# RWKV's bonus product is written into the quarter's own output columns, and the wait for the gate of the second quarter back is dropped

## The chip, the core and the metric

The kernel runs on one core of a Trainium2 chip. A core has five engines that each work through a queue of their own in order: TensorE (PE, matrix products and transposes), VectorE (DVE), ScalarE (ACT), GpSimd (POOL) and SyncE (SP, which here only starts transfers). They wait for one another through semaphores. The metric is device time in microseconds (us) of one execution; lower is better. Several executions are timed and their median is compared. One more execution is recorded by the profiler, and durations and waits are read from that one.

## The reference

One layer of a hybrid recurrent trunk is applied to a prompt of 1024 tokens and, with states that are handed in, to 8 sample sequences of one token each. An input projection feeds three groups of heads: RWKV-7 (6 heads of 64), HGRN2 (6 heads of 64) and RG-LRU (256 channels). Their outputs go side by side through an output projection, a residual sum and an MLP of width 4096. The change touches the last lines of RWKV-7:

```
def step(S, inp):
    rt, wt, kt, vt, kkt, at = inp
    sa = jnp.einsum('bhvk,bhk->bhv', S, -kkt)
    S = S * wt[:, :, None, :] + sa[..., None] * (kkt * at)[:, :, None, :] + vt[..., None] * kt[:, :, None, :]
    return S, jnp.einsum('bhvk,bhk->bhv', S, rt)
...
gn = ((out - mean) * lax.rsqrt(var + GN_EPS)).reshape(B, T, c) * ln_w + ln_b
bonus = (jnp.sum(r_h * k_h * r_k, -1, keepdims=True) * v_h).reshape(B, T, c)
return (gn + bonus) * g, S_T
```

So the output of a token is the normalised scan output plus the bonus (a scalar per head times v), all times the gate g. The bonus needs r, k and v only, and neither the scan nor the gate.

## The kernel before, in words

Channels lie on the 128 partitions, tokens along the free axis. A dense product is made of three float32r products (high by high, high by low, low by high), named `in`, `out`, `up` and `dn` after the projection. The tile `mix[k]` (128 channels, all tokens) holds the layer's input first; once a half of the tokens is normalised and split into high and low parts, the same columns take the output of the head groups (RWKV has `mix[0]` to `mix[2]`), and later the residual stream.

The tokens of the prompt are taken in two halves of 512. RWKV cuts these once more: a *quarter* is 256 tokens of one pair of heads, in four *chunks* of 64. There are 12 quarters, numbered q = 0 to 11 in the order half, pair, quarter of the half (`PARTS`). A quarter named `1_0` on PE rows is half 1, first quarter. Four generators work on it:

- `rw_operands(q)` (line 515 on) makes the operands: decay, normalised keys, transposed keys and values (`vT`, `bt`, `kt`), and last, behind `yield D8`, the bonus: a product of PE (`bonus`), then a multiplication by v on DVE into the tile `bo`. It then releases the quarter's inputs and signals `A2`.
- `rw_inverse(q)` waits for `A2` and builds the inverse of a triangular matrix for each chunk (`sc`, `W`, `Y`), then signals `B`. Two streams share the quarters, even and odd.
- `rw_chain(q)` waits for `B` and carries the state through the four chunks: three dependent products a chunk (`ch` from `st,az`, from `rh,yz`, from `mv,bt`), each followed by a small DVE operation (lines 714, 718, 727). Then come 48 small products for the quarter's output, and it signals `C`.
- `rw_finish(q)` waits for `C`, normalises, transposes (`oT`), adds the bonus (line 772, which reads `bo` and writes `mix`), multiplies by the gate (`gate` on PE, line 779 on DVE) and signals `P`.

Beside these run HGRN2 (`hgrn`, which also does the sample part), RG-LRU (`lru`), and as the *filler* the dense products of the input projections and of the output projection (`projections`, `out_proj`). Near its end the filler waits for the last streams: the columns of `mix[2]` and `mix[5]` are split last (`KS`), and the key `("end",)` stands in front of them.

PE's order is written out by `weave`: it keeps a clock of its own, with a cost for each product and a delay (`D1`, `D2` and so on) after each step of a stream, takes whichever stream is due, and lets the filler have the rest. The order of the other engines is set by a scheduler of the tile framework, which looks at priorities (`PRI`).

The buffer `bo` has two copies. The line `if q >= 2: yield ("P", q - 2)` keeps `rw_operands` from asking for a third before the second quarter back has used its own and has gone through its gate. Until then this stream does nothing else, so the operands of the next quarter wait as well.

Of the kernel before, what the change touches and what calls it, by code (L numbers as in the profile page):

```python
# [17 lines left out]
P = 128  # L18
# [7 lines left out]
HT = 512  # L26
HW = HT + NB
QT = 256
# [24 lines left out]
def kernel(ctx: ExitStack, tc: tile.TileContext, i, o):  # L53
# [18 lines left out]
    def mm(out, lhsT, rhs, start=True, stop=True):  # L72
        n, m = rhs.free_size(), lhsT.free_size()
        now[0] += n / 2400 if rhs.dtype == F32R else 0.19 if n < 16 else max(n, m) / (600 if m > 64 else 800)
        PE.matmul(out, lhsT, rhs, start=start, stop=stop)  # L75

    def tr(out, in_, idn):
        now[0] += 0.11
        PE.transpose(out, in_, idn)
# [3 lines left out]
    def bank_o(name):  # L83

        while now[0] < o_busy[0]:
            yield o_busy[0] - now[0]
        return ps("o", name)

    def used_o(delay=L_O):
        o_busy[0] = now[0] + delay  # L90

    def ev(key, delay=1.5):
        done[key] = now[0] + delay
# [51 lines left out]
    mix = [mixp.tile([P, TP], F32, name=f"mix{k}") for k in range(KT)]  # L145
# [39 lines left out]
    def vec(name, k, n=1):  # L185
        return vt[:, at[name] + k:at[name] + k + n]
# [66 lines left out]
    def head_inv_root(sq, n, name, floor, tmp):  # L253

        pc = yield from bank_o(f"pc_{name}")
        nt = n // P
        for t in range(nt):
            mm(pc[:, 2 * t:2 * t + 2], sq[:, t * P:(t + 1) * P], bones2)
        used_o()
        a = small.tile([P, 2 * nt], F32, tag="ir_kk", name=f"ir_{name}", bufs=1)  # L260
        V.tensor_scalar(a, pc[:, :2 * nt], floor, None, op0=ALU.max)
        rpow(a)

        V.tensor_copy(tmp.rearrange("p (x c) -> p x c", c=64), bc(a[:, :, None], [P, 2 * nt, 64]))
        yield D1
        pb = yield from bank_o(f"pb_{name}")
        for t in range(nt):
            tr(pb[:, t * P:(t + 1) * P], tmp[:, t * P:(t + 1) * P], ident)
        used_o()
        return pb[:, 0:n]  # L270
# [231 lines left out]
    def w2(tag, n, bufs=2, name=None):  # L502
        return rwp.tile([P, QT], F32, tag=tag, name=f"{name or tag}_{n}", bufs=bufs)
# [7 lines left out]
    def twice(ap):  # L511

        return bc(ap.rearrange("p (c t) -> p c t", t=C)[:, :, None, :], [P, ap.shape[1] // C, 2, C])

    def rw_operands(q):

        j, hf, qt = PARTS[q]
        n = f"{j}_{hf}_{qt}"
        q0 = qt * QT
        qs = slice(q0, q0 + QT)  # L520
        jc = slice(j * P, (j + 1) * P)
        yield ("lora", hf)
        yield ("rkv", j, hf)
        xwa, _ = lora[hf]
        r, k, v = rkv[j, hf]

        def ck(ap):
            return ap.rearrange("p (c t) -> p c t", t=C)

        def heads_of(out, pt):  # L530

            for h, b in enumerate(brow):
                S.copy(out[b], pt[b].rearrange("p (c h x) -> p c h x", h=2, x=C)[:, :, h])

        r_, k_, v_ = r[:, qs], k[:, qs], v[:, qs]
        t1, t2, t3, t4 = (w2(f"t{u}", n, 1) for u in range(1, 5))

        act(t2, k_, AF.Square, scale=vec("kk", j))

        pw = yield from bank_o(f"pw_{n}")  # L540
        mm(pw[:, 0:QT], wup[:, jc], xwa[:, qs])
        used_o()
        act(t1, pw[:, 0:QT], AF.Tanh, bias=hw0[:, j:j + 1], scale=0.5)
        V.tensor_scalar(t1, t1, -DECAY, -DECAY, op0=ALU.mult, op1=ALU.add)
        yield D4
        pn = yield from head_inv_root(t2, QT, f"kk{n}", 1e-24, t4)
        V.scalar_tensor_tensor(t4, k_, vec("kk", j), pn, op0=ALU.mult, op1=ALU.mult)
        V.tensor_tensor_scan(t2, rmask_f, t1, 0.0, op0=ALU.mult, op1=ALU.add)
        yield D5
        pa = yield from bank_o(f"pa_{n}")  # L550
        mm(pa[:, 0:QT], aup[:, jc], xwa[:, qs])
        used_o()
        act(t3, pa[:, 0:QT], AF.Tanh, bias=ha0[:, j:j + 1], scale=0.5)
        if q >= 3:
            yield ("C", q - 3)
        if q >= 1:
            yield ("sc", q - 1)
        yield D6
        ee = rwp.tile([P, NQ, C + 1], F32, tag="ee", name=f"ee_{n}", bufs=1)
        wc = rwp.tile([P, NQ], F32, tag="wc", name=f"wc_{n}", bufs=3)  # L560
        ar = rwp.tile([P, NQ, 2, C], F32, tag="ar", name=f"ar_{n}", bufs=3)
        bt = rwp.tile([P, NQ, P], F32, tag="bt", name=f"bt_{n}", bufs=3)
        kt = rwp.tile([P, NQ, C], F32, tag="kt", name=f"kt_{n}", bufs=1)
        vr = rwp.tile([P, NQ, C], F32, tag="vr", name=f"vr_{n}", bufs=3)
        G.memset(ee[:, :, 0:1], 1.0)
        act(ee[:, :, 1:C + 1], ck(t2), AF.Exp)
        act(t1, t2, AF.Exp, scale=-1.0)
        V.tensor_copy(wc, ee[:, :, C])

        pt = yield from bank_o(f"vT_{n}")  # L570
        S.copy(bt.rearrange("p c (h t) -> p c h t", t=C), twice(v_))
        for c in range(NQ):
            tr(pt[:, c * P:(c + 1) * P], bt[:, c], ident)
        used_o()
        heads_of(vr, pt)
        V.scalar_tensor_tensor(t2, t3, 1.0, t4, op0=ALU.add, op1=ALU.mult)
        for h, b in enumerate(brow):
            V.scalar_tensor_tensor(kz[b, 0, :, h], ck(t2[b]), 0.5, ck(t1[b]), op0=ALU.mult, op1=ALU.mult)
        V.tensor_scalar(t3, t3, hka[:, j:j + 1], omka[:, j:j + 1], op0=ALU.mult, op1=ALU.add)
        V.tensor_tensor(t3, t3, k_, op=ALU.mult)  # L580
        for h, b in enumerate(brow):
            V.tensor_tensor(kz[b, 1, :, h], ck(t3[b]), ck(t1[b]), op=ALU.mult)
        V.scalar_tensor_tensor(ar[:, :, 0, :], ck(t4), -1.0, ee[:, :, 0:C], op0=ALU.mult, op1=ALU.mult)
        V.tensor_tensor(ar[:, :, 1, :], ck(r_), ee[:, :, 1:C + 1], op=ALU.mult)
        ev(("A", q), L_OPS)
        V.scalar_tensor_tensor(t2, r_, vec("rk", j), t3, op0=ALU.mult, op1=ALU.mult)
        yield D7

        pt = yield from bank_o(f"bt_{n}")
        for c in range(NQ):  # L590
            tr(pt[:, c * P:(c + 1) * P], kz[:, 0, c].rearrange("p h t -> p (h t)"), ident)
        used_o()
        S.copy(bt, pt.rearrange("p (c x) -> p c x", x=P))
        yield D4
        pt = yield from bank_o(f"kt_{n}")
        for c in range(NQ):
            tr(pt[:, c * P:(c + 1) * P], kz[:, 1, c].rearrange("p h t -> p (h t)"), ident)
        used_o()
        heads_of(kt, pt)
        if q >= 2:  # L600
            yield ("P", q - 2)
        yield D8
        bo = w2("bo", n)
        pb = (yield from bank_o(f"bonus_{n}"))[:, 0:QT]
        mm(pb, bones, t2)
        used_o()
        V.tensor_tensor(bo, pb, v_, op=ALU.mult)
        if qt == 1:
            free["pm"] += 3
        live[q] = dict(wc=wc, ar=ar, bt=bt, kt=kt, vr=vr, bo=bo)  # L610
        ev(("A2", q), L_EV)
        yield D9
# [812 lines left out]
    with tc.manual_schedule(engines={mybir.EngineType.PE}):  # L1425
        start()
        dense_work = projections()
        weave([each(rw_chain, *NP), each(rw_inverse, *NP[0::2]), each(rw_inverse, *NP[1::2]), each(rw_operands, *NP), each(rw_finish, *NP), hgrn(),
               each(lru, *((t, hf) for hf in range(2) for t in range(2)))], dense_work)
        done["end",] = now[0]  # L1430
        phase0.close()
        nhp = ctx.enter_context(tc.tile_pool(name="nhp", bufs=1, side="right", reuse_waits="tile"))
        nh0, nl0 = ([nhp.tile([P, HT], F32R, name=f"{q}0_{k}") for k in range(KT)] for q in ("nh", "nl"))
        for c0, n in CH[1:]:
            acc[c0] = nhp.tile([P, 264], F32, name=f"acc{c0}")
        weave([norms()], dense_work, to_the_end=True)
# [159 lines left out]
```

## Time and profile before

| what | value |
|---|---|
| time, median of 3 (lowest to highest) | 1594.51 us (1593.97 to 1595.9) |
| the profiled execution's own time | 1596.51 us |
| its span, first to last instruction | 1594.7 us |
| mean clock granted to PE | 0.972 |
| PE busy | 1504.8 us (94% of the span) |
| DVE, ACT, POOL busy | 769.9, 663.4, 381.5 us (48%, 42%, 24%) |

A row of the timeline gives the start of a piece in us from the start of the span, its duration, the engine, the line, the operation, what it writes and reads, its shape and how many instructions it holds; in brackets stands how long the engine sat idle before it, and what released it. A row of the windows gives the busy time of each engine in a stretch, with the number of instructions, then the clock that was granted to PE (1.00 is full speed), the share of the DMA engines and GB/s. PE's products overlap, so the durations of rows sum to more than the time they take; the distance between starts is the time one takes.

### The profile page before, as it was taken

How to read it: one execution, taken by the hardware profiler on the slowest of the kernel's cores; microseconds unless marked ns; L12 is line 12 of the kernel's file. 1: busy time of each engine (PE TensorE's matmuls, PEld its weight loads, DVE VectorE, ACT ScalarE, POOL GpSimd, SP SyncE). 2: the span in 40 equal slices, each digit the busy share in tenths (PEclk: the TensorE clock that was granted, in tenths of full speed). 3: DMA queues.
4: the chain of work that ended last, by engine and by line, in shares of the span. 5: the costliest groups of instructions: out<-in, count | busy, mean ns of one | idle time of the engine just before them, and what ended most of it. 6: DMA issues, size and time to landing. Idle time of an engine off the chain costs nothing.

```text
span 1594.7 us, 30262 instructions
## 1 busy us (share of the span) xinstructions
PE 1504.8 (94%) x12536; PEld 1324.2 (83%) x12536; DVE 769.9 (48%) x1799; ACT 663.4 (42%) x1435; POOL 381.5 (24%) x531
## 2 busy tenths in 40 slices
PE   8979998999999988899798999999999999999997
PEld 6757777898888877777697989899999998989887
DVE  7777676666655865764465322222222222222224
ACT  3544745655464562553244424233232423233232
POOL 4553322333334343223222010101111010111011
PEclk9989999999999998899899999999999999999999
DMA  4324442443433432226133443545454454444242
GB/s 164 125 55 105 97 92 68 106 93 70 106 68 95 102 80 74 56 68 153 34 120 93 106 93 80 106 80 106 80 106 80 101 98 91 95 91 95 54 92 107
DMA packets 53081, 146.89 MB, mean 92 GB/s; under 512 B 6960, under 2 KB 7248, under 8 KB 52944
## 3 DMA queue, kind: packets, MB, share of 16 engines
q0 software_dynamic: 22976, 65.33, 24.8%
q1 hardware_dynamic: 29824, 79.61, 15.4%
q8 instruction: 98, 1.61, 0.4%
q14 instruction: 39, 0.32, 0.1%
q10 hardware_dynamic: 144, 0.04, 0.0%
HBM read 138.87 MB, written 6.07 MB: 91 GB/s over the span
## 4 chain that ended last, share of the span: by engine, by line
PE 72%; DVE 8%; DMA 6%; ACT 6%; issue 5%; POOL 3%; SPq 0%; POOLq 0%; ACTq 0%; DVEq 0%
PE up L75 22%; PE dn L75 20%; PE in L75 13%; PE ch L75 3%; PE out L75 3%; PE W L75 2%; PE Y L75 2%; DMA wl_in<-in_w_in 1%; DMA raw_in<-in_w_in 1%; PE gram L75 1%; PE sc L75 1%; DMA raw_out<-in_w_out 1%; DMA raw_w<-in_w 1%; POOL mix L363 1%; ACT wh_in L280 1%
## 5 line engine op out<-in xcount | busy, mean ns | idle before, releaser
L75 PE MATMUL in<-xh,wl_in 128*128 128x512 f32 (+3 forms) x648 | 221.6, 342 | 5.2 <-DMA wl_in<-in_w_in 3.8
L75 PE MATMUL in<-xl,wh_in 128*128 128x512 f32 (+3 forms) x648 | 221.9, 342 | 3.2 <-DVE xl L374 3.2
L75 PE MATMUL dn<-hh,wl_w 128*128 128x264 f32 (+2 forms) x696 | 222.9, 320 | 0.3 <-DMA wl_w<-in_w 0.3
L75 PE MATMUL dn<-hl,wh_w 128*128 128x264 f32 (+2 forms) x696 | 222.8, 320 | 0.0
L75 PE MATMUL in<-xh,wh_in 128*128 128x512 f32 (+3 forms) x648 | 222.3, 343 | 0.5 <-ACT praw_wa L421 0.5
L75 PE MATMUL dn<-hh,wh_w 128*128 128x264 f32 (+2 forms) x696 | 222.6, 320 | 0.0
L1484 DVE TENSOR_TENSOR mix<-mix,dn 128x512 f32<-128x512 f32 (+2 forms) x192 | 98.4, 512 | 241.9 <-PE dn L75 241.9
L285 POOL DMA_DIRECT2D wl_w<-in_w x86 | 76.0, 887 | 573.3 <-ACT hh L1414 305.8
L280 ACT ACTIVATE wh_w<-raw_w 128x512 fp32r<-128x512 f32 (+1 forms) x90 | 70.6, 785 | 283.6 <-PE dn L75 227.4
L1413 DVE SCALAR_TENSOR_TENSOR rl<-up,rl 128x512 f32<-128x512 f32 (+2 forms) x96 | 49.6, 516 | 205.3 <-ACT rl L1412 205.2
L75 PE MATMUL up<-nxh,wh_w 128*128 128x264 f32 (+1 forms) x512 | 145.6, 284 | 0.0
L75 PE MATMUL up<-nxl,wh_w 128*128 128x264 f32 (+1 forms) x512 | 144.8, 283 | 0.4 <-POOL nxl L1310 0.4
L75 PE MATMUL up<-nxh,wl_w 128*128 128x264 f32 (+1 forms) x512 | 145.0, 283 | 0.0
L75 PEld LDWEIGHTS dn<-hh,wl_w 128*128 128x128 f32 x696 | 130.8, 188 | 13.1 <-DMA wl_w<-in_w 2.8
L75 PEld LDWEIGHTS in<-xh,wl_in 128*128 128x128 f32 x648 | 126.4, 195 | 16.8 <-DMA wl_in<-in_w_in 4.8
L75 PEld LDWEIGHTS in<-xl,wh_in 128*128 128x128 f32 x648 | 126.6, 195 | 16.4 <-DVE xl L374 6.6
L75 PEld LDWEIGHTS dn<-hl,wh_w 128*128 128x128 f32 x696 | 130.9, 188 | 10.1
L75 PEld LDWEIGHTS dn<-hh,wh_w 128*128 128x128 f32 x696 | 131.0, 188 | 9.4
L75 PEld LDWEIGHTS in<-xh,wh_in 128*128 128x128 f32 x648 | 126.4, 195 | 11.3 <-issue 1.2
L75 PE MATMUL up<-nh,wh_w 128*128 128x512 f32 x256 | 101.7, 397 | 0.0
L75 PE MATMUL up<-nh,wl_w 128*128 128x512 f32 x256 | 101.5, 396 | 0.0
L75 PE MATMUL up<-nl,wh_w 128*128 128x512 f32 x256 | 101.4, 396 | 0.0
(459 smaller groups left out, 3285.1 us busy)
## 6 DMA issues: line engine op xcount, KB each, us to landing
raw_in<-in_w_in SPq DMA_DIRECT2D x53, 512.0 KB, 3.3
wl_in<-in_w_in POOLq DMA_DIRECT2D x43, 512.0 KB, 5.6
raw_w<-in_w SPq DMA_DIRECT2D x32, 512.0 KB, 3.3
raw_w<-in_w SPq DMA_DIRECT2D x64, 256.0 KB, 2.6
wl_w<-in_w POOLq DMA_DIRECT2D x58, 256.0 KB, 4.1
wl_w<-in_w POOLq DMA_DIRECT2D x28, 512.0 KB, 5.5
raw_out<-in_w_out SPq DMA_DIRECT2D x16, 512.0 KB, 3.3
out_y_prompt<-yt SPq DMA_DIRECT2D x16, 256.0 KB, 2.0
```

The costliest lines, as they stand in the source:

```text
L75: PE.matmul(out, lhsT, rhs, start=start, stop=stop)
L280: act(wh[:, ks], raw[:, ks], AF.Copy)
L285: G.dma_start(wl[:, ks], src[:, ks], accum_op=ALU.add)
L363: G.tensor_tensor(x, x, rs, op=ALU.mult)
L1413: V.scalar_tensor_tensor(rl[:, :n], pt[:, :n], 0.0, rl[:, :n], op0=ALU.max, op1=ALU.mult)
L1484: V.tensor_tensor(x2[m][:, c0:c0 + n], x2[m][:, c0:c0 + n], pt[:, :n], op=ALU.add)
```

## The change

The bonus gets no tile of its own. It is written where the quarter's output will stand, into the columns of `mix[j]`, and line 772 adds the normalised scan output in place (`live[q]` carries the view under the name `bo` as before, so `rw_finish` keeps its text). The wait for `("P", q - 2)` goes.

```
         used_o()
         heads_of(kt, pt)
-        if q >= 2:
-            yield ("P", q - 2)
         yield D8
-        bo = w2("bo", n)
+
+        bo = mix[j][:, hf * HT + q0:hf * HT + q0 + QT]
         pb = (yield from bank_o(f"bonus_{n}"))[:, 0:QT]
         mm(pb, bones, t2)
         used_o()
         V.tensor_tensor(bo, pb, v_, op=ALU.mult)
```

No instruction is added or taken away on any engine; SP's transfers keep their order, and the orders of PE, DVE, ACT and POOL change from the third quarter on, until the last quarter's output products. Three places show how.

The first is on PE, where the order first differs: the first quarter of the second pair (`bonus` from `t_1_0_0`), while the dense products of an input projection run. Before, its bonus product stands 19 rows behind the gate product of the first quarter of all, in the middle of the second quarter's chain (`ch_0_1`):

```order
L75 MATMUL in_0_0_1937<-xh_228,wl_in_0_1862 128x512
L75 MATMUL in_0_0_1937<-xh_229,wh_in_0_1861 128x512
L75 MATMUL in_0_0_1937<-xl_237,wh_in_0_1861 128x512
L75 MATMUL in_0_0_1937<-xh_229,wl_in_0_1862 128x512
L75 MATMUL in_0_0_1937<-xh_230,wh_in_0_1861 128x512
L75 MATMUL bonus_0_0_1969<-t_1_0_0_1432,bones 128x256
L75 MATMUL ch_0_1_1854<-mv_0_1_1174,bt_0_1_934 128x64
L75 MATMUL in_0_0_1937<-xl_238,wh_in_0_1861 128x512
```

With the change it stands right behind the output products of the first quarter (`ch_0_0`), and the first products of its inverse (`sc`) and the next quarter's operands (`pw`) follow eight dense products later:

```order
L75 MATMUL ch_0_0_1315<-vr_0_0_660,sr_0_0_805 64x64
L75 MATMUL bonus_0_0_1814<-t_1_0_0_1430,bones 128x256
L75 MATMUL in_0_0_1681<-xh_225,wh_in_0_1506 128x512
L75 MATMUL in_0_0_1681<-xl_233,wh_in_0_1506 128x512
L75 MATMUL in_0_0_1681<-xh_225,wl_in_0_1507 128x512
L75 MATMUL in_0_0_1681<-xh_226,wh_in_0_1506 128x512
L75 MATMUL in_0_0_1681<-xl_234,wh_in_0_1506 128x512
L75 MATMUL in_0_0_1681<-xh_226,wl_in_0_1507 128x512
L75 MATMUL in_0_0_1681<-xh_227,wh_in_0_1506 128x512
L75 MATMUL in_0_0_1681<-xl_235,wh_in_0_1506 128x512
L75 MATMUL sc_1_0_0_1849<-ar_0_0_1558,kz 128x128 x4
L75 MATMUL pw_0_1_1857<-pm_wa_419,wup 128x256
```

The bonus moved 74 rows forward, and all that waits for it moved with it.

The second place is PE at the end of the woven stretch, where the last dense products that do not need the last quarter (`out_768`) run out and the chain of the last quarter (`ch_1_1`) is left alone. Before:

```order
L75 MATMUL out_768_9157<-mh_9043,wh_out_1_9065 128x264
L75 MATMUL out_768_9157<-ml_9051,wh_out_1_9065 128x264
L75 MATMUL out_768_9157<-mh_9043,wl_out_1_9066 128x264
L75 MATMUL ch_1_1_9125<-mv_1_1_8608,bt_1_1_8179 128x64
L75 MATMUL ch_1_1_9125<-st_2_1_1_9182,az 128x64
L75 MATMUL ch_1_1_9125<-rh_2_1_1_9188,yz 128x64
L75 MATMUL ch_1_1_9125<-mv_1_1_8608,bt_1_1_8179 128x64
L75 MATMUL ch_1_1_9125<-st_2_1_1_9193,az 128x64
L75 MATMUL ch_1_1_9125<-rh_2_1_1_9199,yz 128x64
L75 MATMUL ch_1_1_9125<-mv_1_1_8608,bt_1_1_8179 128x64
L75 MATMUL ch_1_1_9125<-st_2_1_1_9204,az 128x64
L75 MATMUL ch_1_1_9125<-rh_2_1_1_9210,yz 128x64
```

(one more `mv,bt` product follows, then the 24 rows of small products). With the change:

```order
L75 MATMUL out_768_9172<-mh_9076,wl_out_1_9102 128x264
L75 MATMUL out_768_9172<-mh_9078,wh_out_1_9101 128x264
L75 MATMUL out_768_9172<-ml_9086,wh_out_1_9101 128x264
L75 MATMUL out_768_9172<-mh_9078,wl_out_1_9102 128x264
L75 MATMUL out_768_9172<-mh_9079,wh_out_1_9101 128x264
L75 MATMUL ch_1_1_8950<-mv_1_1_8219,bt_1_1_7947 128x64
L75 MATMUL out_768_9172<-ml_9087,wh_out_1_9101 128x264
L75 MATMUL out_768_9172<-mh_9079,wl_out_1_9102 128x264
L75 MATMUL ch_1_1_8950<-st_2_1_1_9190,az 128x64
L75 MATMUL ch_1_1_8950<-rh_2_1_1_9198,yz 128x64
L75 MATMUL ch_1_1_8950<-mv_1_1_8219,bt_1_1_7947 128x64
L75 MATMUL ch_1_1_8950<-st_0_183,ar_1_1_7946 64x64
```

Ten chain products stood behind the last dense one, now three do: two whole chunks and one product moved in among the dense products.

The third place is DVE just ahead of that, where the low parts `ml` of the output projection's input are made (line 1234 before, 1233 with the change). Before, the chain of the last but one quarter (`ch_1_0`) ends between them:

```order
L282 TENSOR_TENSOR wl_out_1_8917<-raw_out_1_8915,wh_out_1_8916 128x1024
L718 COPY mv_1_0_7982<-ch_1_0_8597 128x64
L1234 TENSOR_TENSOR ml_9044<-mix_69,mh_9036 128x520
L1245 TENSOR_TENSOR acc_7896<-acc_7896,sq_0_8912 128x512
L1234 TENSOR_TENSOR ml_9045<-mix_70,mh_9037 128x520
L727 SCALAR_TENSOR_TENSOR st_0_183<-ch_1_0_8597,wc_1_0_7278,ws_2_1_0_8948 128x64
L1234 TENSOR_TENSOR ml_9047<-mix_72,mh_9039 128x520
```

With the change the last quarter's chain (`ch_1_1`) is there, in its second chunk:

```order
L713 TENSOR_TENSOR rh_2_1_1_9040<-ch_1_1_8950,mv_1_1_8219 128x64
L1244 TENSOR_TENSOR acc_8181<-acc_8181,sq_0_9021 128x512
L1233 TENSOR_TENSOR ml_9081<-mix_70,mh_9073 128x520
L1233 TENSOR_TENSOR ml_9083<-mix_72,mh_9075 128x520
L1233 TENSOR_TENSOR ml_9084<-mix_73,mh_9076 128x520
L717 COPY mv_1_1_8219<-ch_1_1_8950 128x64
L1233 TENSOR_TENSOR ml_9086<-mix_75,mh_9078 128x520
L1233 TENSOR_TENSOR ml_9087<-mix_76,mh_9079 128x520
L1237 TENSOR_TENSOR mix_76<-out_0_9032,xr_0_9030 128x512
L726 SCALAR_TENSOR_TENSOR st_2_1_1_9063<-ch_1_1_8950,wc_1_1_7945,ws_2_1_1_9064 128x64
```

The copy `mv` now stands behind three `ml` and one `acc` in a row, where it had one operation of another kind ahead of it.

Between the two bonus products of a pair stand, in rows of DVE, 73 to 101 rows before and 48 to 71 with the change (second pair on); between the last of one pair and the first of the next 106 to 122 before, and 93 to 188 with the change.

More of the change, by code (lines that the diff above doesn't have):

```diff
@@ L599, in rw_operands @@
         heads_of(kt, pt)
-        if q >= 2:
-            yield ("P", q - 2)
         yield D8
-        bo = w2("bo", n)
+        bo = mix[j][:, hf * HT + q0:hf * HT + q0 + QT]
         pb = (yield from bank_o(f"bonus_{n}"))[:, 0:QT]
```

## Prediction

> **What bounds the kernel now.** I read the windows first, cut where the work changes its kind.
>
> ```profile
> core 0: us, PE busy (x) PEld busy (x) DVE busy (x) ACT busy (x) POOL busy (x), PEclk, DMA share, GB/s
> 0.00:180.00 180.00, 160.84 (x1240) 125.82 (x1241) 130.86 (x277) 90.36 (x182) 76.63 (x125) 0.96 0.38 107
> 180.00:774.00 594.00, 550.44 (x6193) 481.31 (x6192) 380.69 (x1014) 309.59 (x773) 193.74 (x274) 0.96 0.39 89
> 774.00:797.00 23.00, 13.15 (x89) 10.47 (x88) 6.49 (x22) 3.44 (x17) 3.79 (x9) 0.69 0.01 2
> 797.00:858.00 61.00, 54.82 (x389) 51.72 (x389) 38.32 (x70) 25.74 (x46) 15.91 (x18) 0.95 0.39 122
> 858.00:1595.00 737.00, 725.53 (x4632) 654.85 (x4631) 213.52 (x419) 234.31 (x418) 91.48 (x107) 0.99 0.44 91
> ```
>
> PE is the bound nearly everywhere; no other engine is near its limit over a whole stage. Up to 180 us the order of PE is unchanged, and from 858 us on it is the MLP. So the change can act on two stretches only: 180 to 774 us, where PE is idle for 594 - 550.4 = 43.6 us in small pieces, and 774 to 797 us, where 23 us pass with 89 matmuls and no transfer to speak of. Next I read what the wait that goes had cost, in PE rows of the timeline for the last two quarters.
>
> ```profile
> 617.03 0.60 PE L79 MATMUL kt<-ident,kz 128*128 128x128 f32 x4
> 657.81 0.59 PE L75 MATMUL gate<-pm_xg,gup 128*128 128x256 f32 x2
> 662.19 0.59 PE L75 MATMUL bonus<-t,bones 128*128 128x256 f32 x2
> 698.02 0.60 PE L79 MATMUL kt<-ident,kz 128*128 128x128 f32 x4
> 713.13 1.22 PE L75 MATMUL gate<-pm_xg,gup 128*128 128x256 f32 x2
> 720.14 0.59 PE L75 MATMUL bonus<-t,bones 128*128 128x256 f32 x2
> ```
>
> The transposed keys, the step just ahead of the bonus, are there at 617 and 698 us; the bonus comes at 662 and 720 us, 4 to 7 us after the gate of the second quarter back. So the operands stream stood still for 45 and 22 us. PE did dense products meanwhile: the wait costs nothing where it stands. It costs what it makes late, and that shows at the end:
>
> ```profile
> 774.26 0.28 PE L75 MATMUL out<-mh,wl_out 128*128 128x264 f32 x1
> 774.38 0.33 PE L75 MATMUL ch<-mv,bt 128*128 128x64 f32 x2
> 775.09 0.43 PE L75 MATMUL ch<-st,az 128*128 128x64 f32 x2 [0.38 <-DVE st L727]
> 777.47 0.43 PE L75 MATMUL ch<-st,az 128*128 128x64 f32 x2 [0.45 <-DVE st L727]
> 779.86 0.69 PE L75 MATMUL ch<-st,az 128*128 128x64 f32 x2 [0.45 <-DVE st L727]
> 783.00 0.47 PE L75 MATMUL ch<-st,ar 64*64 64x64 f32 x2 [0.45 <-DVE st L727]
> 795.93 0.70 DVE L1234 TENSOR_TENSOR ml<-mix,mh 128x520 fp32r<-128x520 f32 x1 [0.70 <-ACT mh L1233]
> 796.07 0.56 PE L75 MATMUL out<-mh,wh_out 128*128 128x256 f32 x1
> ```
>
> The dense work that needs nothing of the last quarter is out at 774.3. Then the last quarter's chain runs by itself, PE and DVE in turn, its products and its finish follow, and the output projection goes on at 796.1. I call this stretch the tail.
>
> **The change, part by part.** *The tail.* Before, three whole chunks of the last chain stand behind the last dense product, and with the change one does (second place in the section on the change). What leaves the tail are the chunks from 775.09 to 777.47 and from 777.47 to 779.86, which is 4.77 us. Their six PE steps now stand among the dense products and take PE's time there. What one takes, a row of an earlier chain shows:
>
> ```profile
> 741.34 0.39 PE L75 MATMUL out<-mh,wh_out 128*128 128x512 f32 x1
> 741.56 0.39 PE L75 MATMUL out<-ml,wh_out 128*128 128x512 f32 x1
> 741.79 0.33 PE L75 MATMUL ch<-st,az 128*128 128x64 f32 x2
> 741.93 0.48 PE L75 MATMUL out<-mh,wl_out 128*128 128x512 f32 x1
> 742.25 0.40 PE L75 MATMUL out<-mh,wh_out 128*128 128x512 f32 x1
> ```
>
> From 741.56 to 742.25 are 0.69 us for two dense products (0.23 each, by the starts ahead) and one chain step: 0.23 for the step, and 6 x 0.23 = 1.4 us given back. Their DVE and POOL operations run beside dense work.
>
> *The clock in the tail.* The third chunk took 783.00 - 779.86 = 3.14 us where the two before took 2.4. The windows say why:
>
> ```profile
> 374.00:377.00 3.00, 0.75 (x8) 0.54 (x8) 2.93 (x5) 2.94 (x8) 2.63 (x4) 0.92 0.84 150
> 377.00:381.00 4.00, 4.00 (x28) 2.85 (x29) 3.70 (x14) 0.95 (x4) 1.17 (x2) 0.63 0.01 1
> 774.00:780.00 6.00, 3.46 (x20) 2.50 (x18) 2.08 (x8) 0.00 (x0) 1.37 (x5) 0.94 0.00 0
> 780.00:787.00 7.00, 5.02 (x54) 4.27 (x54) 0.73 (x3) 0.81 (x7) 1.15 (x3) 0.56 0.03 7
> ```
>
> PE's granted clock falls to 0.56 some 5.6 us after the dense work is out. With the change the chunk that remains is done about 0.7 + 2.4 = 3.1 us after it, ahead of that fall: another 3.14 - 2.39 = 0.75 us. The products and the finish behind it stay in the slow stretch, as before. The Trainium skill, in "TensorE: Matmul & The Clock Gate", Part 1, says that the clock is halved after an idle window of about 3.4 us and restored after a busy one, and that the windows run freely. By it the fall follows the idle time and not the chunk, which goes with the sum of -4.1 below; if the clock were low from the start of the tail, it would be -3.4. The trace agrees about the half clock, but it fell at 377 us after only 2.3 us idle, so the measured distance is what I use.
>
> *The order between 180 and 774 us.* The same instructions stand there in another order, so work that PE waited for may come sooner or later. What PE waited for in it:
>
> ```profile
> PE ch L75 <- DVE rh L714: 6.0, 5, 2.8
> PE ho L75 <- DVE hst L1050: 5.6, 9, 1.0
> PE ch L75 <- DVE st L727: 5.5, 10, 1.2
> PE pb_kk L79 <- DVE t L264: 4.7, 4, 2.8
> ...
> PE ch L75 <- DVE mv L718: 3.2, 4, 1.3
> ...
> PE Y L75 <- ACT wm L662: 2.3, 1, 2.3
> PE pc_kk L75 <- ACT t L543: 2.2, 1, 2.2
> PE gate L75 <- DVE mix L772: 2.2, 1, 2.2
> PE W L75 <- DVE xm L687: 1.4, 1, 1.4
> ```
>
> Without the HGRN2 row (`ho`) these are RWKV's: 6.0 + 5.5 + 4.7 + 3.2 + 2.3 + 2.2 + 2.2 + 1.4 = 27.5 us. None is the wait that goes; they are small misses between a PE product and the DVE or ACT result for it, 27 events of about 1 us. The dense products that the order puts between dependent products are about as many after as before, so I take nothing for this term. Its bounds are -9 (a third of the 27.5 us goes) and +11 (three more stalls of the kind in the rival below).
>
> *The write into `mix`.* Twelve products change their target, and 24 additions one source:
>
> ```profile
> L772 DVE SCALAR_TENSOR_TENSOR mix<-oT,vt,bo x24: 434/484/492, 186.1 to 792.9; 64x256 f32<-64x256 f32 x24
> L607 DVE TENSOR_TENSOR bo<-bonus,pm_v x12: 411/425/454, 75.1 to 720.8; 128x256 f32<-128x256 f32 x12
> L779 DVE SCALAR_TENSOR_TENSOR mix<-mix,vt,gate x12: 475/480/482, 191.1 to 794.8; 128x256 f32<-128x256 f32 x12
> ```
>
> Line 779 already does in place and into `mix` what line 772 will, in the same 0.48 us on twice the partitions, so the price is nil; at the worst the twelve products would take 0.48 instead of 0.425 us, 0.7 us in all, and none of them is in the tail. The readers of those columns (the squares, the split into high and low parts) are over long before: RWKV's inputs are made from them. No transfer moves past SP's queue; on POOL the small operations of the same stream move with it.
>
> Sum: -4.77 + 1.4 - 0.75 = -4.1 us. The profiled execution took 1596.5 us, so the same execution would take 1592.4. It lies 2.0 us above the median shown, and against the median of 1594.5 the forecast is 1590.4.
>
> **The rivals.** *Slower, because quarters clump.* Without the wait, the two quarters of a pair follow each other closely, and then the stream waits for the next pair's projections: 48 to 71 DVE rows between the two bonus products of a pair where 73 to 101 were, then up to 188 to the next. Operands and inverses of two quarters then load DVE and ACT at once, and PE, which takes its products in order, stalls. The place is every pair from the second on; the price is in the windows above: from 374 to 377 us DVE and ACT were busy for 2.9 of 3 us, PE for 0.75, and the clock behind it fell to 0.63 for 4 us, so 2.25 + 0.37 x 4 = 3.7 us for one such stall. Above one more of these than before the gain is gone, and from (4.1 + 3.2) / 3.7 = two on the kernel is slower by more than 0.2%. With three the time is 1590.4 + 11.1 = 1601.5. For it: the place on DVE where `mv` now stands behind three `ml` and an `acc`, with only eight dense products of 0.23 us to cover it; 0.7 us each, by the row of `ml` above, make 2.8. Against it: the instructions are the same, DVE is busy for 381 of 594 us, and the stretches between the clumps get emptier. The Trainium skill, in "TensorE: Matmul & The Clock Gate", Part 1, calls DVE and ACT strict queues that never reorder; the trace shows nothing against it.
>
> *Faster still.* A bonus that comes earlier also spreads chain, inverse and finish further from the results they wait for; a third of the 27.5 us would give 1590.4 - 9 = 1581. Against it: the cover of the chain steps grows by little.
>
> *No change: the gain is given back.* If the stretch behind the tail were set by transfers that start on their own, the output projection would go on at the same time as before. Against it: transfers are idle in the tail (share 0.01), since the weight buffers are still held by the two output tiles that wait for the last quarter; they start when the tail ends, whenever that is. Or one stall of 3.7 us cancels the sum. Time 1594.5.
>
> *It doesn't do what it says.* If another wait took the gate's place, such as a reader of `mix`, the order on the chip would show a late bonus again. In the new program the product on DVE waits for PE alone. Time 1594.5.
>
> **How the numbers follow.** Forecast 50%, quarters that clump 21%, faster still 12%, given back 14%, not as said 3%. A measurement of this kernel can tell about 0.2%, 3.2 us, from no change. The forecast of -4.1 with a spread of a few us from the reordering leaves it 41 points faster and 9 within; so faster is 41 + 12 = 53%, the same 9 + 14 + 3 = 26%, slower 21%. The range runs from 1579, the faster rival with 2 us to spare, to 1602, the three stalls; it leaves out worse clumping, the rest of the 2 in 10. The forecast's own range is 1586 to 1594.
>
> **What would show it.** In the new profile the bonus should follow `kt` within about 4 us in every quarter. The tail, from the last dense product to the next, should be 21.8 - 5.5 = 16 us long, with one chunk of 2.4 us in it. Idle time of PE between 180 us and the tail near 43.6 us keeps the forecast; 50 or more, with DVE full around it and half-clock windows behind, is the clumping. The forecast falls if the tail keeps its length, if `mv` or `rh` of the last chain hold up the dense products by more than 3 us, or if the stretch from the tail's end to 858 us grows by what the tail lost.

## The result, and the profile after

| | before | after |
|---|---|---|
| median of 4 (lowest to highest) | 1594.24 us (1592.11 to 1595.9) | 1613.49 us (1610.82 to 1615.38) |
| span of the profiled execution | 1594.7 us | 1613.6 us |
| mean clock granted to PE | 0.972 | 0.962 |

The changed kernel takes 1.0122 times as long, with a 95% interval from 1.0107 to 1.0138. The forecast was 1590.4, the range ended at 1602: the kernel got slower by 19 us where 4 us less were foretold.

The windows of the changed kernel are cut where its own work changes its kind (columns as in the windows of before):

```profile
core 0: us, PE busy (x) PEld busy (x) DVE busy (x) ACT busy (x) POOL busy (x), PEclk, DMA share, GB/s
0.00:180.00 180.00, 161.85 (x1252) 127.88 (x1253) 132.31 (x283) 88.28 (x180) 77.68 (x124) 0.94 0.38 106
180.00:801.70 621.70, 564.25 (x6198) 496.02 (x6196) 384.67 (x1016) 311.21 (x774) 200.39 (x278) 0.93 0.37 85
801.70:816.00 14.30, 7.09 (x71) 5.73 (x69) 4.07 (x14) 3.33 (x17) 2.25 (x4) 0.80 0.01 3
816.00:878.00 62.00, 57.42 (x401) 54.33 (x401) 40.74 (x76) 26.59 (x49) 16.86 (x19) 0.94 0.37 120
878.00:1613.60 735.60, 724.01 (x4622) 652.60 (x4620) 211.58 (x415) 233.45 (x416) 89.60 (x106) 1.00 0.44 92
```

For a comparison that ends exactly at the last dense product, these are the two middle windows of the kernel before, cut at 774.3 and 796.1 us:

```profile
180.00:774.30 594.30, 550.74 (x6196) 481.61 (x6195) 380.99 (x1014) 309.59 (x773) 193.74 (x274) 0.96 0.39 89
774.30:796.10 21.80, 12.01 (x86) 9.62 (x84) 5.59 (x21) 3.44 (x17) 3.57 (x8) 0.69 0.01 2
```

The tail got shorter, from 21.8 to 14.3 us. The stretch ahead of it grew from 594.3 to 621.7 us, by 27.4, with the same products in it but for the chain steps that moved there (6196 and 6198 records; a few are missing in a trace). Of the 27.4 us, 13.9 are idle time of PE (594.30 - 550.74 = 43.6 before, 621.70 - 564.25 = 57.5 after) and 13.5 are busy time. The clock can account for most of the latter: the trace's records of the granted clock hold 44 us at half speed in this stretch before and 85 us after, which fits the mean of 0.93 (0.07 x 621.7 / 0.5 = 87); 41 us more at half speed are worth up to 20. With the tail, 27.4 - 7.5 = 19.9 us; the two executions lie 18.9 us apart, and the stages behind account for the rest.

PE rows of the timeline show the bonus of the last two quarters in the changed kernel:

```profile
658.69 0.60 PE L79 MATMUL kt<-ident,kz 128*128 128x128 f32 x4
661.00 0.59 PE L75 MATMUL bonus<-t,bones 128*128 128x256 f32 x2
687.04 0.79 PE L75 MATMUL gate<-pm_xg,gup 128*128 128x256 f32 x2 [2.60 <-DVE mix L771]
693.49 0.66 PE L79 MATMUL kt<-ident,kz 128*128 128x128 f32 x4
696.01 0.59 PE L75 MATMUL bonus<-t,bones 128*128 128x256 f32 x2
```

The bonus now follows the transposed keys by 2.3 and 2.5 us, where it came 45 and 22 us behind them; in all twelve quarters the distance is 2.3 to 4.3 us. Neither of the two stands right behind the gate of the second quarter back any more (these gates start at 639.5 and 687.0 us). The change does what it says. It does not bring the first of the two forward in time, though: the bonus comes at 661.0 us where it came at 662.2, since the transposed keys ahead of it come 41.7 us later than before.

The tail, in PE rows of the timeline of the changed kernel:

```profile
801.56 0.28 PE L75 MATMUL out<-mh,wl_out 128*128 128x264 f32 x1
802.00 0.43 PE L75 MATMUL ch<-st,az 128*128 128x64 f32 x2
804.38 0.33 PE L75 MATMUL ch<-st,ar 64*64 64x64 f32 x2 [0.45 <-DVE st L726]
805.88 0.28 PE L75 MATMUL ch<-vr,sr 64*64 64x64 f32 x2
810.98 1.25 PE L79 MATMUL oT<-ident,ot 128*128 128x128 f32 x4 [4.82 <-DVE ot L762]
815.95 0.56 PE L75 MATMUL out<-mh,wh_out 128*128 128x256 f32 x1
```

One chunk of 2.38 us is left behind the last dense product, as foretold. From the start of that product to the start of the next one (801.56 to 815.95 us) the tail is 14.4 us long; the tables below give it in this way.

What PE waited for from 180 us to the last dense product (the waits of PE: sum, times, longest, in us):

```profile
PE ch L75 <- DVE st L726: 12.7, 10, 4.0
PE vT L79 <- ACT t L553: 6.8, 2, 3.6
PE ho L75 <- DVE hst L1049: 6.2, 8, 1.3
PE W L75 <- DVE xm L686: 5.9, 3, 3.8
PE out L75 <- DMA wl_out<-in_w_out: 4.3, 2, 4.0
PE rows_sa L75 <- DVE s_tm L840: 4.0, 1, 4.0
PE gate L75 <- DVE mix L771: 3.0, 2, 2.6
PE in L75 <- DMA wl_in<-in_w_in: 2.5, 1, 2.5
```

Read the last column here, not the sum. In the kernel before the longest wait of the whole list was 2.8 us. Now seven of these eight rows have single waits of 2.5 to 4.0 us. Counted over the stretch, PE stood still for 1.5 us or more 7 times before (16.7 us together) and 14 times after (37.9 us).

Two of the 14 are read here. The first is on ACT, in its rows of the timeline of the changed kernel:

```profile
379.53 1.04 ACT L284 ACTIVATE wl_in<-wh_in 128x1024 fp32r<-128x1024 f32 x1
380.59 1.28 ACT L923 ACT_TABLE_LOAD   x1
381.88 0.81 ACT L923 ACTIVATE lf<-lf,fB,fA 128x512 f32<-128x512 f32 x1
382.71 1.28 ACT L553 ACT_TABLE_LOAD   x1
384.01 0.47 ACT L553 ACTIVATE t<-pa,ha 128x256 f32<-128x256 f32 x1
```

RWKV's tanh (line 553), for which PE stands still, lies behind a logarithm of HGRN2 (line 923), and each of the two loads a table: 1.04 + 1.28 + 0.81 + 1.28 us pass on ACT before it starts. The row of PE that waits, and the windows of the same kernel around it:

```profile
384.54 1.12 PE L79 MATMUL vT<-ident,bt 128*128 128x128 f32 x4 [3.63 <-ACT t L553]
```

```profile
380.50:383.70 3.20, 0.41 (x3) 0.19 (x1) 1.78 (x4) 3.15 (x4) 2.61 (x3) 1.00 0.35 137
383.70:390.00 6.30, 4.20 (x18) 3.89 (x18) 5.76 (x13) 3.35 (x10) 1.99 (x2) 0.50 0.51 85
390.00:400.80 10.80, 10.67 (x70) 10.14 (x71) 6.72 (x19) 3.45 (x5) 2.10 (x4) 0.50 0.21 69
```

From 383.7 us, near the end of the idle time of 3.63 us, the clock is at half for 17.1 us. A second stall, of 1.40 us, lies in this stretch (at 388.7 us), but for its last 10.8 us PE is busy. What the half clock costs is seen on dense products of one shape, inside the stretch and behind it:

```profile
386.11 0.42 PE L75 MATMUL in<-xh,wl_in 128*128 128x264 f32 x1
386.33 0.42 PE L75 MATMUL in<-xh,wh_in 128*128 128x264 f32 x1
403.13 0.28 PE L75 MATMUL in<-xh,wh_in 128*128 128x264 f32 x1
403.25 0.29 PE L75 MATMUL in<-xl,wh_in 128*128 128x264 f32 x1
```

One takes 0.22 us, by the distance of the starts, where it takes 0.12 at full clock.

The second is on DVE, in its rows of the timeline of the changed kernel:

```profile
701.24 0.69 DVE L1233 TENSOR_TENSOR ml<-mix,mh 128x512 fp32r<-128x512 f32 x1
701.85 1.22 DVE L282 TENSOR_TENSOR wl_out<-raw_out,wh_out 128x1024 fp32r<-128x1024 f32 x1
702.98 0.42 DVE L630 TENSOR_TENSOR sa<-sc,cmask 128x256 f32<-128x256 f32 x1
703.32 0.41 DVE L630 TENSOR_TENSOR sr<-sc,cmask 128x256 f32<-128x256 f32 x1
703.65 0.43 DVE L686 STREAM_TRANSPOSE xm<-ym 128x256 f32<-128x256 f32 x1
```

```profile
700.40:704.30 3.90, 0.11 (x3) 0.10 (x4) 3.85 (x9) 0.39 (x2) 0.00 (x0) 1.00 0.06 15
```

The inverse's transpose (`xm`, line 686) stands behind the split of the output projection's input (`ml`), the split of a weight tile (`wl_out`) and two operations for the next inverse. DVE is full (3.85 of 3.9 us) and PE gets 0.11 us of work. Three more of the long stalls end on DVE. At 604.9 us (3.96 us long) a scan of RG-LRU and an addition of HGRN2 stand ahead of the chain's state; at 684.4 us (2.60 us) a weight split, RG-LRU and HGRN2 stand ahead of the tile that the gate product waits for; at 641.0 us (4.04 us) it is HGRN2 and, there, operands of RWKV too. Two (2.5 and 4.0 us) end with the transfer of a weight tile. As far as the stalls were read, then, they are collisions: a result for which PE waits stands in a queue behind work that, for the most part, other streams put there. The other seven were not read.

### The profile page after: what moved, and what is told of

Same layout as the page of the kernel before. It is cut to its first block, busy times and chain, and to the rows that moved or that the text cites. A ratio compares the mean times of both kernels' runs of the same rounds, so it can differ in the third digit from the quotient of the medians.

```text
span 1613.6 us, 30275 instructions
## 1 busy us (share of the span) xinstructions
PE 1514.6 (94%) x12536; PEld 1336.5 (83%) x12536; DVE 773.4 (48%) x1799; ACT 662.9 (41%) x1435; POOL 386.8 (24%) x531
## 4 chain that ended last, share of the span: by engine, by line
PE 69%; DVE 9%; ACT 7%; issue 6%; DMA 5%; POOL 4%; POOLq 0%; ACTq 0%; DVEq 0%
PE up L75 21%; PE dn L75 20%; PE in L75 12%; PE out L75 3%; PE ch L75 3%; PE W L75 2%; PE Y L75 1%; DMA raw_in<-in_w_in 1%; PE gram L75 1%; PE sc L75 1%; DMA raw_out<-in_w_out 1%; ACT wh_in L280 1%; POOL mix L363 1%; ACT gsq L757 1%; DMA wl_out<-in_w_out 1%
## 5 line engine op out<-in xcount | busy, mean ns | idle before, releaser
L75 PE MATMUL in<-xh,wl_in 128*128 128x512 f32 (+3 forms) x648 | 225.7, 348 | 3.9 <-DMA wl_in<-in_w_in 2.5
L75 PE MATMUL in<-xl,wh_in 128*128 128x512 f32 (+3 forms) x648 | 226.7, 350 | 1.8 <-DVE xl L374 1.7
L75 PEld LDWEIGHTS in<-xl,wh_in 128*128 128x128 f32 x648 | 130.0, 201 | 14.4 <-DVE xl L374 4.2
L75 PEld LDWEIGHTS in<-xh,wl_in 128*128 128x128 f32 x648 | 129.9, 201 | 14.1 <-DMA wl_in<-in_w_in 2.7
L75 PEld LDWEIGHTS in<-xh,wh_in 128*128 128x128 f32 x648 | 129.9, 201 | 9.4 <-issue 0.5
```

## Theories

Three accounts of the 27 us fit this profile.

- **Clumps.** Without the wait the quarters run together, whatever the rest of the order is. The loss is a cost of the change, and each wait that is given back takes a share of it away.
- **Starts.** Without the wait the first quarter of a pair begins when its projections arrive, together with HGRN2's run and the sample part, and collides with them. This, too, is a cost of the change.
- **The order drawn.** The planner writes one long order, and any shift early in it moves everything behind. Each such order has its own set of collisions, and the time scatters from one to the next by far more than the change is worth. The changed kernel drew a bad one. The loss goes if the order is drawn anew, with the wait still left out. In the expectations of e2 to e7 this account is narrower: the planner's delays fit the order of before, and any other order costs about 1%. It took the form given here only after these runs.

## Experiments: the wait given back, whole and by halves

The first kernel writes the bonus into `mix[j]` as the changed kernel does, and has the wait again:

```
         heads_of(kt, pt)
+        if q >= 2:
+            yield ("P", q - 2)
         yield D8
```

> The changed kernel with the wait for the gate of the second quarter back put in again: the bonus alone moves from its own tile into the output columns. Every engine's order is that of before. If the wait's going is the cause of the 19 us, this takes the time of before, 1594 us within 3, with a tail of 21.8 us. If writing the bonus into the output columns costs something (a dependence on other users of the columns, a slower operation), it keeps some of the loss, 1600 us or more.

It took 1593.55 us (10 runs) against 1592.6 us for the kernel before (13 runs), a ratio of 1.0 (0.9987 to 1.0012). On every engine its order is that of the kernel before. Its windows, cut at its last dense product and at the end of its tail:

```profile
180.00:772.10 592.10, 549.34 (x6197) 479.42 (x6197) 381.12 (x1014) 310.43 (x775) 193.77 (x274) 0.97 0.39 90
772.10:793.90 21.80, 12.02 (x85) 9.63 (x84) 5.59 (x21) 3.44 (x17) 3.56 (x8) 0.70 0.01 2
```

Idle time (42.8 us) and tail (21.8 us) are those of before. The write into `mix` costs nothing; all of the difference comes with the wait and the order that follows from it.

The next two give the wait back to one quarter of each pair only (`qt` is 0 for the first and 1 for the second). This is e2; e3 has `qt == 1` in its place:

```
+        if q >= 2 and qt == 0:
+            yield ("P", q - 2)
```

> The changed kernel with the wait for the first quarter of each pair only. Theory of clumps (the second quarter follows the first too closely): the second quarter still follows at once, so most of the loss stays, 1606 to 1614 us. Theory of the starts (the first quarter of a pair now starts at the moment its projections arrive, together with HGRN's run and the sample part): the stream is held back ahead of that start as before, so the loss goes, 1592 to 1600 us. Theory of the order (the table of delays fits the order of before, and any other order costs about 1%): 1600 to 1614 us.

> The changed kernel with the wait for the second quarter of each pair only. Theory of clumps: the second quarter is spread from the first as before, so most of the loss goes, 1592 to 1600 us. Theory of the starts: the first quarter of a pair comes later than in the changed kernel and no longer waits for its projections, 1594 to 1602 us. Theory of the order: 1600 to 1614 us.

| wait for | time, us (runs) | ratio to before (95%) | tail, us | idle, 180 us to last dense product | at half clock there |
|---|---|---|---|---|---|
| both (e1) | 1593.55 (10) | 1.0 (0.9987 to 1.0012) | 21.8 | 42.8 | 34 |
| first (e2) | 1582.28 (4) | 0.9918 (0.9893 to 0.9942) | 18.9 | 40.1 | 38 |
| second (e3) | 1583.11 (4) | 0.9928 (0.991 to 0.9946) | 22.9 | 40.0 | 31 |
| none (the change) | 1613.49 (4) | 1.0122 (1.0107 to 1.0138) | 14.4 | 57.5 | 85 |

Leaving out either half of the wait makes the kernel 10 to 11 us faster than e1 and takes 3 us of idle time away. Leaving out both makes it 20 us slower. A cost that each missing wait brings with it would not do that. In e3 the gain is not even in the tail, which is 1 us longer. No expectation for e2 or e3 was met: both times lie below every range, of which the lowest began at 1592 us. The narrow account, by which any order but that of before costs 1%, is wrong, since two other orders are faster. What is left of it is that the time scatters with the order, but three orders are few.

## Experiments: the same two kernels in other orders

PE's order hangs on the planner's cost of a dense product, `n / 2400`. Another number there changes no instruction, only the order. It was set to 2300, 2350, 2375, 2425, 2450 and 2500, in the kernel before and in the changed one:

```
-        now[0] += n / 2400 if rhs.dtype == F32R else ...
+        now[0] += n / 2350 if rhs.dtype == F32R else ...
```

> Before, with one number of the planner changed: the cost it assumes for a dense product, by 2% (columns by 2350 in place of 2400 a us). No wait changes. Theory of the order: the planner's table of delays fits one order, and this other order costs several us, 1600 us or more. Theories of clumps and of starts: the wait still spreads the quarters, so within 5 us of before, 1590 to 1599 us.

> Before, with the planner's cost of a dense product 2% lower (2450 columns a us). Theory of the order: another order than the one the table of delays fits, 1600 us or more. Theories of clumps and of starts: 1590 to 1599 us.

> The changed kernel with the planner's cost of a dense product 2% higher (2350 columns a us). Theory of the order: an arbitrary order, as likely better as worse than the changed kernel's, 1600 to 1620 us, about where the reordered kernels with the wait lie. Theories of clumps and of starts: it stays at 1608 to 1618 us, clearly above the reordered kernels with the wait.

> The changed kernel with the planner's cost of a dense product 2% lower (2450 columns a us). Theory of the order: 1600 to 1620 us, about where the reordered kernels with the wait lie. Theories of clumps and of starts: 1608 to 1618 us, clearly above the reordered kernels with the wait.

> Before, planner's cost of a dense product 4% higher (2300 columns a us), a further draw of the order with the wait. Theory of the order: the wait matters only through the order it leads to, so this lies anywhere from 1575 to 1602 us, with a tail of 21 to 23 us. Theories of clumps and of starts: with the wait PE's idle time from 180 us to the last dense product stays under the 57 us of the changed kernel in each draw, and the mean of such draws lies well below that of draws without the wait.

> The changed kernel, planner's cost of a dense product 4% higher (2300 columns a us), a further draw of the order without the wait. Theory of the order: anywhere from 1570 to 1615 us, with a tail of 12 to 15 us, and at equal idle time ahead of the tail some 7 us faster than a draw with the wait. Theories of clumps and of starts: idle time ahead of the tail is above that of the draw with the wait.

> Before, planner's cost of a dense product 1% lower (2425 columns a us), a further draw with the wait. Theory of the order: 1575 to 1602 us, tail 21 to 23 us. Theories of clumps and of starts: less idle time ahead of the tail than the draw without the wait at the same number.

> The changed kernel, planner's cost of a dense product 1% lower (2425 columns a us), a further draw without the wait. Theory of the order: 1570 to 1615 us, tail 12 to 15 us. Theories of clumps and of starts: more idle time ahead of the tail than the draw with the wait at the same number.

> The kernel before with the planner's number 2375. Both theories: another draw of the order, 1570 to 1605, tail 20 to 23 us.

> The changed kernel with 2375. Tail 12 to 15 us. Theory of the order: 1565 to 1600, on the mean of the pairs some 4 us below the kernel before with the same number, with a spread of 15 us either way. Theory of clumps: slower than the kernel before with the same number by 10 us or more.

> The kernel before with the planner's number 2500. Another draw of the order: 1570 to 1605, tail 20 to 23 us.

> The changed kernel with 2500. Tail 12 to 15 us. Theory of the order: 1565 to 1600. Theory of clumps: slower than the kernel before with the same number by 10 us or more.

Each of these was timed once; the kernel before itself ranged from 1589.4 to 1599.3 us over all its runs, so a single time is good to about 5 us. The row of 2400 has the medians of four. "Last dense" is the start of the last dense product ahead of the tail.

| planner's number | time with / without the wait, us | difference | tail, us | last dense, us | idle from 180 us | half clock there |
|---|---|---|---|---|---|---|
| 2300 | 1590.89 / 1576.85 | -14.0 | 20.3 / 12.5 | 769.5 / 768.1 | 43.4 / 42.9 | 38 / 24 |
| 2350 | 1600.60 / 1576.46 | -24.1 | 21.8 / 13.5 | 776.9 / 765.1 | 46.0 / 34.7 | 44 / 41 |
| 2375 | 1583.35 / 1588.61 | +5.3 | 22.6 / 13.2 | 765.1 / 777.3 | 41.5 / 46.4 | 24 / 51 |
| 2400 | 1594.24 / 1613.49 | +19.3 | 21.8 / 14.4 | 774.3 / 801.6 | 43.6 / 57.5 | 44 / 85 |
| 2425 | 1574.07 / 1570.32 | -3.8 | 22.6 / 12.5 | 755.7 / 759.1 | 37.4 / 35.8 | 34 / 41 |
| 2450 | 1576.67 / 1584.52 | +7.9 | 22.1 / 12.5 | 756.7 / 774.2 | 34.4 / 43.6 | 41 / 58 |
| 2500 | 1594.82 / 1592.68 | -2.1 | 24.0 / 12.5 | 772.7 / 781.7 | 43.7 / 49.0 | 55 / 55 |

Three things follow. First, the order alone scatters the time by far more than the change was thought to be worth: over 26.5 us with the wait and over 43 us without it. Second, the changed kernel at 2400 is the slowest of all fourteen; without the wait the other six draws take 1570 to 1593 us. Third, the tail is 7 to 12 us shorter without the wait in all seven pairs.

Many expectations were missed on the way. The times of e5, e6 and e7 lie below every range set for them (the lowest began at 1590 us). From e8 on the ranges were wide, drawn up with these times known, so a time inside them says little; e10 (1574.07 us) still fell below its range by 1 us, and the tails of e8 and e16 were off by about 1 us. What counts against the clumps is that by that account e15 and e17 were to be 10 us or more slower than their partners with the wait; they are 5.3 us slower and 2.1 us faster.

The traces also show how close the quarters of a pair run. Between the two bonus products of a pair, from the second pair on, lie 48.7 us on the mean in the kernel before and 35.5 us in the changed one. So the quarters do clump. But in the other six orders without the wait it is 32.0 to 34.3 us, closer still, and these kernels are 21 to 43 us faster than the changed one. The clumping by itself does not make the order of 2400 slow.

The mean of the seven differences is -1.7 us, with a 95% interval of 13 us on either side, and their median is -2.1. So whether the change gains or loses apart from the draw can't be told from these runs. The shorter tail (9.2 us on the mean) is partly given back: the last dense product comes 8.0 us later on the mean, with 12 us on either side. Some of that is the chain's steps that moved there. Whether the rest is a small general cost of going without the wait, or chance, stays open.

## Experiments: where the loss sits

Two kernels keep the changed kernel's own order in the first part and draw it anew behind that. The planner's number becomes 2425 or 2350 only once its clock is past 270; PE's order is that of the changed kernel up to about 365 and 330 us.

```
-        now[0] += n / 2400 if rhs.dtype == F32R else ...
+        now[0] += n / (2425 if now[0] > 270 else 2400) if rhs.dtype == F32R else ...
```

> The changed kernel with its own order on TensorE up to about 365 us (the planner's number becomes 2425 only from planner clock 270 on). Theory of the order (the loss is this draw's row of collisions between 180 us and the last dense product): the two stalls near 273 and 384 us or at least the first of them stay, those of the changed kernel near 609, 645, 687 and 704 us go or move; idle time of TensorE from 180 us to the last dense product comes down from 57.5 to 38 to 50 us, time 1570 to 1600. Theory of clumps (without the wait the quarters run together whatever the order): the idle time stays above 52 us, time 1605 or more. If the loss sat ahead of 365 us, the time stays above 1600 with the idle time behind 365 us little changed.

> The same with 2350 from planner clock 270 on; TensorE's order is the changed kernel's up to about 330 us. Theory of the order: idle time from 180 us to the last dense product 36 to 50 us, time 1570 to 1600. Theory of clumps: above 52 us, time 1605 or more.

They took 1587.61 and 1601.2 us (once each; the kernel before, timed beside them, 1597.92). The windows of the changed kernel, cut at 365 us:

```profile
180.00:365.00 185.00, 174.29 (x2050) 147.93 (x2049) 127.30 (x326) 107.14 (x258) 57.89 (x84) 1.00 0.41 89
365.00:801.70 436.70, 389.96 (x4150) 348.10 (x4148) 257.37 (x692) 204.08 (x516) 142.50 (x194) 0.90 0.36 84
```

and of the kernel with 2425 from there on:

```profile
180.00:365.00 185.00, 174.22 (x2046) 147.69 (x2046) 127.40 (x326) 106.64 (x258) 57.62 (x84) 1.00 0.40 88
365.00:779.50 414.50, 376.84 (x4212) 337.46 (x4210) 260.39 (x696) 204.41 (x519) 145.25 (x198) 0.94 0.38 89
779.50:789.10 9.60, 4.04 (x16) 3.13 (x16) 3.03 (x10) 3.18 (x17) 1.04 (x1) 0.75 0.00 0
```

Up to 365 us the two are alike (10.7 and 10.8 us idle). Behind it the idle time falls from 436.70 - 389.96 = 46.7 to 37.7 us and the busy time by 13 us, and the time spent at half clock falls from 85 to 48 us. The same cut in the kernel before gives 8.9 us idle ahead of 365 us and 34.7 behind it, though it is not quite at the same place in its work there (1932 records of PE ahead of the cut, against 2050). So about 2 us of the lost idle time sit ahead of 365 us and 12 behind, and 9 of those 12 go when the order is drawn anew, without the wait. The new order has collisions of its own: its longest stall, 5.09 us at 642.6 us, is longer than any of the changed kernel's.

The kernel with 2350 missed its expected time by 1 us (1601.2 for at most 1600). Its idle time of 46.5 us lies where the order's theory put it, and below the 52 us of the clumps.

One wait stayed in both kernels: that of `vT` for the tanh behind HGRN2's logarithm (3.61 and 3.42 us). In the kernel with 2425 this PE row of the timeline shows it:

```profile
385.74 0.47 PE L79 MATMUL vT<-ident,bt 128*128 128x128 f32 x1 [3.61 <-ACT t L553]
```

Here too the half clock lasts 17.1 us, and here too a second stall of 1.40 us lies in it; in the kernel with 2350, where no second stall over 1 us follows, it lasts 6.8 us and comes back for 3.4. The collision stands 17 us or more behind the place where the orders part, so the new draws left it as it was.

## Experiment: the fastest version once more

The fastest of the draws, the changed kernel with 2425, was timed five more times.

> The changed kernel with 2425 once more, in rounds: 1568 to 1574 against the kernel before at 1592 to 1596, a ratio of 0.984 to 0.988.

It took 1566.83 us (1562.99 to 1568.15, 5 runs) against 1592.1 us for the kernel before (8 runs): 0.9834 times, with a 95% interval from 0.9818 to 0.9851. It is faster than both kernels, and slightly below the expected 1568 to 1574 us and 0.984 to 0.988. Its windows:

```profile
180.00:759.10 579.10, 543.81 (x6188) 477.57 (x6187) 382.52 (x1010) 308.43 (x769) 194.82 (x279) 0.97 0.39 91
759.10:771.50 12.40, 5.95 (x66) 5.01 (x66) 3.29 (x11) 3.33 (x17) 1.62 (x2) 0.80 0.02 4
```

PE is idle for 35.3 us where the changed kernel at 2400 had 57.5, and the tail is as short as the change makes it. Most of the gain is the draw: the kernel before took 1574.07 with the same number.

## Why the prediction was wrong, step by step

- **What bounds the kernel**: right about the place, since the stretch ahead of the tail and the tail itself are where the two kernels differ. But what grew there is not PE's idle time alone, as it reads the stretch: 13.5 of the 27.4 us are busy time, most of which the half clock can account for.
- **The tail**: the mechanism was right, the size too small. It was to lose 4.77 + 0.75 = 5.5 us and lost 7.4. The one chunk took 2.38 us, as foretold. The missing 2 us are in the steps around it: 0.4 us less between the last dense product and `st,az` (774.26 to 775.09 before, 801.56 to 802.00 after), and 1.5 us less from the first output product to the output projection (783.00 to 796.07 before, 804.38 to 815.95 after). I had said that the products behind the chunk stay in the slow stretch. They don't: they are done by 806 us, and the half clock comes at 810.3 us. That is 8.7 us behind the start of the last dense product, where the records of the kernel before have it 5.0 us behind (the 5.6 us were read from windows), so this distance is no constant.
- **The steps given back (1.4 us)**: they can't be seen by themselves in a stretch that changed by 27 us.
- **The order between 180 and 774 us**: this is the step that failed. "The dense products that the order puts between dependent products are about as many after as before, so I take nothing for this term", it said, with bounds of -9 and +11. The stretch grew by 27.4 us; less the 1.4 us of the moved steps, the term was some +26. The average cover says nothing on single collisions, and the loss shows in those: 14 stalls of 1.5 us or more in place of 7 (37.9 us in place of 16.7), and 41 us more at half clock. e1 shows that this came with the wait and not with the write, and the sweep that other orders without the wait do not have it. The bounds were too narrow as well. I had worked them out from the waits of one order; the seven orders with the wait alone lie 26.5 us apart.
- **The write into `mix`**: right. The multiplication into `mix` took 424 ns where the one into `bo` took 425 (medians of twelve), and e1 shows no difference in time.
- **Slower, because quarters clump**: its signs were there (idle time above 50 us, DVE full, half-clock windows), and its price for one stall, 3.7 us, looks near the mark: 27.4 us over seven more stalls is 3.9 each. That is in part luck, since the idle time in shorter waits fell by 7.3 us meanwhile. It reckoned with three more stalls where there were seven, and the cause it named does not set this order apart from the faster ones. Of the two stalls read above, one has HGRN2's logarithm in front and the other the output projection's splits, not the operands of a second quarter. And the other orders without the wait clump as much or more, and five of the six have no more than 46.4 us of idle time from 180 us to the last dense product.
- **No change**: wrong for the tail. The output projection went on later than before only because the dense work ahead of the tail ended later.
- **It doesn't do what it says**: ruled out by the bonus rows.

The forecast of -4.1 us was for the change in an order that stays as good as it was. The mean over seven orders, -1.7 with 13 us on either side, doesn't contradict that, but it doesn't show it either.

## What to carry to other kernels

Where a planner writes the order, a wait taken out is a new draw of the whole order behind it: price that step by how far several orders of the same kernel lie apart (here 26.5 us of 1590), not by counting instructions between dependent ones. Judge such a change by pairs over several draws, since one pair can show any sign; here it was +19 in one and -24 in another. And before a better schedule is sought by argument, a sweep of one planner number may give more than the change: here 1.7% for both together.

## What the hardware showed that I had not expected

Short stalls can cost a second time through the clock, and their length alone does not say whether they do. These windows of the changed kernel show an idle time of 1.30 us with 3.4 us at half clock behind it, and the two windows of 3.4 us across which a stall of 3.20 us lies (269.7 to 272.9 us), which brought no half clock at all:

```profile
425.80:427.10 1.30, 0.05 (x1) 0.00 (x0) 1.30 (x4) 0.63 (x1) 0.00 (x0) 1.00 0.00 0
428.00:431.40 3.40, 3.40 (x49) 2.95 (x45) 0.17 (x1) 1.69 (x11) 0.28 (x1) 0.51 0.00 0
267.60:271.00 3.40, 2.11 (x10) 1.39 (x8) 1.90 (x4) 1.98 (x4) 0.19 (x1) 1.00 0.70 137
271.00:274.40 3.40, 1.49 (x9) 1.32 (x10) 1.63 (x5) 3.30 (x19) 1.48 (x2) 1.00 0.00 0
```

The half clock nearly doubles what a product takes here, small ones too: the 64x64 products of a quarter's output start every 0.029 us ahead of 428.0 us and every 0.053 us behind it. The stall of 3.63 us at 381 us was the dearest: 17.1 us at half clock among dense products, though PE was busy for 10.67 of the last 10.8 us of it. The half-clock stretches here last 3.4, 6.8, 10.2, 13.7 or 17.1 us, which are multiples of one window of 3.4 us, and from 180 us to the end of the tail those of one execution all start on one grid of such windows. The Trainium skill, in "TensorE: Matmul & The Clock Gate", Part 1, gives windows of that length that run freely, which agrees; it lets a whole idle window bring the half clock and one busy window end it, and neither holds in the rows shown here. What decides it stays open: PE was busy for 2.1 us in the window of the grid ahead of 428.0 us, and for 2.11 and 1.49 us in the two windows around the stall of 3.20 us.
